# Two gate chunks moved from beside the last attention to beside the state space part

## The chip, the cores and the metric

The kernel runs on one core of a Trainium2 chip, in one launch. The metric is device microseconds of the execution, lower is better. Engines are named as in the profile: PE multiplies, PEld loads its weights, DVE, ACT and POOL work element by element, SP issues the DMA transfers.

## What is computed

Two blocks one after the other on 1024 tokens of width 1024. The first block (two layers, with a context of 256 tokens) is not touched. The second block is the reference's `second_block`:

```python
xn = rms_norm(h, mix_norm[i])
z = xn @ w_in[i]                                   # 1024 x 3072
q, k, v, gate_a, u, gate_s = jnp.split(z, splits, axis=-1)      # 512 columns each
attn = dilated_mixture_attention(q, k, v, q_norm[i], k_norm[i]) * jax.nn.silu(gate_a)
ssm = s5_glu(u, lambda_re[i], ..., b_glu[i]) * jax.nn.silu(gate_s)
h = h + jnp.concatenate([attn, ssm], axis=-1) @ w_out[i]
```

Queries and keys are normalised by head, the attention has 8 heads of 64. `s5_glu` is a linear recurrence over time in groups of 16 channels, computed as a scan, then Gelu, then a gated projection.

## The kernel before

Numbers are float32, and each product is made from a high and a low part: three matmuls (L236, L237, L238) for one. The projections of the second block go by chunks of 256 columns of `w_in`; the class `Stream` (L274 on) loads one chunk's 1 MB of weights into `raw` (one buffer), splits it into `wh` and `wl` (one set: ACT casts at L210, DVE and POOL subtract at L215, in eight pieces), and loads the next when both halves are split. `Stream.next` hands a chunk out, `Stream.ahead` splits a half of the following one as soon as its half of the set is free. The order of the chunks is the list given to `Stream`: `wspecs(w_in, a, b)` is one entry for every 256 columns.

Kinds of chunks, with the cost that the code yields for them (about a microsecond of PE per unit): queries or keys, `qk_items`, eight tiles of 128 tokens, 2.56 each, with a norm on DVE, POOL and ACT and then two transposes of 0.43 per pair of tiles (L1814), 23.9 in all; values, `v_tok`, eight tiles, 20.5; gates, `all_gates` and `gates`, two halves of 128 columns by two groups of 512 tokens, 5.12 each, 20.5 in all. A gate group is 24 matmuls of 512 columns, a Tanh on ACT (L723), a product on DVE (L724) and a store on SP (L725). The tiles `gth` and `vt` have one buffer in this part (`K.rb = 1`): the next waits for the store of the one before.

Two stages matter. In the first, `weave` runs the state space part `space()` beside the projections `proj_s()`; in the second it runs the attention `attn_s` beside `side_s()`. `weave` lets that side yield that is behind, by the numbers of `PART`: cost of the one side, cost of the other, a lead of the other, a factor on its cost. So "ssm" goes forward as 134.4 to 159 x 0.982 = 156.1. The chunks of `proj_s` are, in order: two of queries, two of keys, two of values, one of gates. `side_s` has the other three of gates, then the gated projection `glu`, a pause, and one half of the output projection; its lead of 8 puts that much of the gates ahead of the first scores.

The state space part has four blocks (`ssm`). Each counts 5 ahead of its scan (transposes and a product on PE, copied to `s_Z`), then 13 steps of 1.0 on DVE and POOL (L1740 to L1744, no PE), between which the constants of the next block are made (7 more, with some PE work), and 7 behind: products on PE (L1765, L1767), Gelu on ACT (L1769), transposes. The constants of block 0 (7) come ahead of all. The program's order is not strictly that of each engine's queue: when the kernel is built, the framework may put an instruction ahead of one that it takes for not yet ready. Each engine then works its queue in order.

Between the stages the pools change: `sp` (state space) and the six and two banks of PSUM are given up, and the attention's pool `aS` and its four and four banks take their place; the loads of keys and queries stand on SP's queue behind the stores of the values.

Of the kernel before, what the change touches and what calls it, by code (L numbers as in the profile page):

```python
# [20 lines left out]
S = 1024  # L21
# [20 lines left out]
def host_consts():  # L42
# [44 lines left out]
    "low": (27.3, 26, 1.4, 1.0),  # L87
    "m": (171, 105, 13.7, 1.0),
    "d": (176.1, 108, 8.8, 0.96),
    "ssm": (134.4, 159, 0, 0.982),  # L90
    "s": (89.1, 132, 8.0, 1.005),
}
PAUSE = {"d": 0.5, "s": 14.1, "fill": 4.0}
SSM = (2, 4, 6), (1,)
# [320 lines left out]
def wspecs(w, a, b):  # L415
    return [(w[:, c:c + 256], None) for c in range(a, b, 256)]
# [92 lines left out]
def pipe(items, filler=None, part=0.0, young=False):  # L509

    items = iter(items)
    live = []
    while True:
        it = next(items, None)
        if it is not None:
            live.append([it, 0])
        if not live:
            if filler:  # L520
                yield from filler
            return
        loads, front, chain = [], [], []
        for x in live:
            st = x[0][x[1]] or []
            if x[1] == 0:
                loads = st
            elif x[1] == 1:
                front = st
            else:  # L530
                chain = st + chain if young else chain + st
            x[1] += 1
        live = [x for x in live if x[1] < len(x[0])]
        order = [((i + 0.1) / len(front), f) for i, f in enumerate(front)] + [((i + 0.6) / len(chain), f) for i, f in enumerate(chain)]
        for _, f in sorted(order, key=lambda x: x[0]):
            c = f()
            if hasattr(c, "__next__"):
                c = yield from c
            yield c or 1e-6
        for f in loads:  # L540
            f()
        yield 1e-6
        z = 0.0
        while it is None and filler and z < part:
            x = next(filler, None)
            if x is None:
                filler = None
            else:
                z += x
                yield x  # L550
# [178 lines left out]
def all_gates(K, ws, sg, h, ntok, nf):  # L729
    for m2 in range(nf // 2):  # L730
        W = ws.next()
        for m in range(2):
            r = m2 * 2 + m
            yield from gates(K, W, sg[r * P:(r + 1) * P], h, ntok, m)
            ws.ahead(m)
# [1043 lines left out]
def qk_items(K, W, dst, h, gain):  # L1779

    nc = K.nc

    def item(t2):
        rows, st = [], []
        ss = K.small(8, "qns")

        def proj(i):
            t = t2 * 2 + i
            ps = K.w()[:, 0:256]
            c = yield from K.projy(ps, cols(h, t * P, (t + 1) * P), cols(W, 0, 256))  # L1790
            r = K.tp.tile([P, 256], F, tag="qrow", name="qrow", bufs=4)
            nc.scalar.copy(out=r, in_=ps)
            sq = K.tp.tile([P, 256], F, tag="qsq", name="qsq", bufs=2)
            nc.gpsimd.tensor_tensor(out=sq, in0=r, in1=r, op=ALU.mult)
            nc.vector.tensor_reduce(out=ss[:, i * 4:(i + 1) * 4], in_=sq.rearrange("p (h e) -> p h e", h=4), axis=AX.X, op=ALU.add)
            rows.append(r)
            return c

        def norm():
            rr = K.rsqrt(K.mean_eps(ss, 8, 64, "qnm"), 8, "qnr")  # L1800
            for i in range(2):
                r = rows[i].rearrange("p (h e) -> p h e", h=4)
                nc.vector.tensor_tensor(out=r, in0=r, in1=rr[:, i * 4:(i + 1) * 4].unsqueeze(2).to_broadcast([P, 4, 64]), op=ALU.mult)
                if gain is not None:
                    nc.gpsimd.tensor_tensor(out=r, in0=r, in1=gain.unsqueeze(1).to_broadcast([P, 4, 64]), op=ALU.mult)
                s = K.tp.tile([P, 4, 2, 64], FR, tag="qst", name="qst", bufs=2)
                K.split(s[:, :, 0, :], s[:, :, 1, :], r)
                st.append(s)

        def trans(hp):  # L1810
            ps = K.w()
            for h_ in range(2):
                for i in range(2):
                    nc.tensor.transpose(ps[:, (h_ * 2 + i) * P:(h_ * 2 + i + 1) * P], st[i].bitcast(F)[:, hp * 2 + h_].rearrange("p a e -> p (a e)"), K.ident)  # L1814
            o = K.tp.tile([P, 2, 256], F, tag="qo", name="qo", bufs=2)
            nc.scalar.copy(out=o, in_=ps.rearrange("p (h t) -> p h t", h=2))
            nc.sync.dma_start(out=dst[hp * 2:hp * 2 + 2].rearrange("h a e t -> (a e) h t")[:, :, t2 * 256:(t2 + 1) * 256], in_=o)
            return 0.43

        return [None, each(proj, 2), [norm], each(trans, 2)]  # L1820

    for t2 in range(4):
        yield item(t2)
# [179 lines left out]
def stages(K, out):  # L2003
    nc, I = K.nc, K.I
    x, xc = flat(I["x"]), flat(I["ctx"])
# [4 lines left out]
    w_in, w_out, w_ada = flat(I["ev_w_in"]), flat(I["ev_w_out"]), flat(I["ev_w_ada"])  # L2010
# [3 lines left out]
    h = [hp.tile([P, KD, T], FR, name="e_hh"), Slabs([[lo(F, k, c) for c in range(3)] for k in range(KD)], 512)]  # L2014
    rp = K.open("erp")
    ws = Stream(K, "edn", "left", 2, 2, [x for c in range(0, D, 256) for s_ in (0, D) for x in wspecs(w_ada, c + s_, c + s_ + 256)] + [
        x for i, m in enumerate([None, (w_in[:, 0:256], xy_split), (w_in[:, 256:512], xy_split)] + wspecs(w_in, 1792, 2304))
        for x in ([m] if m else []) + wspecs(w_ada, 2 * D + i * 256, min(3 * D, 2 * D + (i + 1) * 256))])
# [88 lines left out]
    for j in range(4):  # L2107
        c = 256 * j
# [27 lines left out]
    sg = [K.dram([512, T], "e_sg%d" % i) for i in range(2)]  # L2136
# [31 lines left out]
    ws = ws2  # L2168
# [121 lines left out]
    h = [hp.tile([P, KD, T], FR, name="o_h" + c) for c in "hl"]  # L2290
    w_in = flat(I["od_w_in"])
# [22 lines left out]
    qd = [K.dram([2, 2, 64, S], "o_qd%d" % i) for i in range(4)]  # L2314
    kd = [K.dram([2, 2, 64, T], "o_kd%d" % i) for i in range(4)]
    vd = [K.dram([T, 512], "o_vd%d" % i) for i in range(2)]
    sg = [K.dram([512, S], "o_sg%d" % i) for i in range(2)]
# [170 lines left out]
    w_in, w_out = flat(I["w_in_2"]), flat(I["w_out_2"])  # L2488
    hp = K.open("shT", "right")
    h = [hp.tile([P, KD, S], FR, name="s_h" + c) for c in "hl"]  # L2490
    ws = Stream(K, "sdn", "right", 1, 1, wspecs(w_in, 2048, 2560) + wspecs(w_in, 0, 2048) + wspecs(w_in, 2560, 3072))
    jk = K.open("sjk", "right")
    FG = jk.tile([P, D], F, name="o_FG")
    nc.sync.dma_start(out=FG, in_=I["final_norm_g"].unsqueeze(0).to_broadcast([P, D]))
# [29 lines left out]
            yield from ssm(K, sp, m, U[m], gT)  # L2524

    def proj_s():
        for dst, gain in ((qd, None), (kd, K.s_gain)):
            for c in range(2):
                W = ws.next()
                yield 0  # L2530
                yield from pipe(qk_items(K, W, dst[c], h, gain))
        for c in range(2):
            yield from v_tok(K, ws, vd[c], h, 8, 4, 64)
        K.tp.release()
        K.tp = K.open("stg", "right")
        yield from all_gates(K, ws, sg[0][0:256], h, S, 2)

    K.pace("ssm")
    weave(K, space(), proj_s(), *PART["ssm"])
    sp.release()  # L2540


    ap = K.open("aS")
# [3 lines left out]
    res = {}  # L2547

    def side_s():
        yield from all_gates(K, ws, sg[0][256:512], h, S, 2)  # L2550
        yield from all_gates(K, ws, sg[1], h, S, 4)
        K.tp.release()
        ws.release()
        hp.release()
        ex = res["ex"] = K.open("sow")
        parts = OutProj.parts(w_out, (1, 0))
        where = [(ex, "raw%d" % i) for i in range(2)]
        raw = [OutProj.fetch(K, where[i], parts[i]) for i in range(2)]
        ws2 = Stream(K, "sge", "right", 1, 2, wspecs(flat(I["w_glu_2"]), 0, 512), 4)
        gl = K.open("sgl", "right")  # L2560
        yield from glu(K, ws2, gl, gT, yd[1])
        gl.release()
        ws2.release()
        so = res["so"] = K.open("so", "right")
        op = res["op"] = OutProj(K, so, where, parts, raw)

        def items():
            for t in range(8):
                xr = {}

                def row(t=t, xr=xr):
                    xr[0] = so.tile([P, D], F, tag="xr", name="xr", bufs=4)
                    nc.sync.dma_start(out=xr[0], in_=x3[t * P:(t + 1) * P])

                def fin(c, ps, t=t, xr=xr):
                    nc.vector.tensor_tensor(out=xr[0][:, c:c + 512], in0=xr[0][:, c:c + 512], in1=ps, op=ALU.add)
                    if c:
                        nc.sync.dma_start(out=xa[t * P:(t + 1) * P, :], in_=xr[0])

                yield op.item(yd[1], sg[1], t, row, fin, t == 7)  # L2580

        g = pipe(items())
        next(g)
        for f in range(2):
            op.ahead(f)
        yield PAUSE["s"]
        yield from g
# [89 lines left out]
```

## Time and profile before

| | us |
|---|---|
| median of three runs | 2837.96 |
| lowest, highest | 2837.86, 2843.56 |
| the profiled execution | 2844.58 |
| its span, first to last instruction | 2842.4 |
| busy in the span: PE, DVE, ACT, POOL | 2483.3, 1745.0, 1172.7, 873.0 |
[...]

The profile is one execution. A row of the windows view gives a stretch by its ends in us from the span's start, its length, then how long each engine was busy in it with the number of its instructions, the granted clock of PE, the DMA engines' busy share and GB/s. The state space stage lies between about 2058 and 2388 us, the last attention between 2388 and 2655. Rows of the waits view give who waited for whom, us in total, times, and the longest. Rows of the timeline give start and length in us, and in brackets how long the engine was idle ahead and for whom. Matmuls are pipelined: their starts tell the pace, not their lengths.

### The profile page before, as it was taken

Reading aid. Unit: us, or ns where it says so; the run is one execution under the profiler, and the core shown is the slowest. Engines: PE = TensorE matmul, PEld = TensorE weight load, DVE = VectorE, ACT = ScalarE, POOL = GpSimd, SP = SyncE. Lnnn points to the kernel's source line nnn. Section 1 sums busy time; section 2 is a strip of 40 time slices with the busy share of each in tenths; the row PEclk is TensorE's granted clock in tenths of the full one; section 3 lists DMA queues with packets and bytes.
Section 4 is the critical chain, followed back from the end, with each engine's and each line's share of the span. In section 5 each row is a group of like instructions: output and inputs, shape, how many; then the busy total and the mean of one; then the engine's idle time right before and its main releaser. Section 6 shows DMA issues by size and latency. Waiting matters only on the chain.

```text
span 2842.4 us, 41920 instructions
## 1 busy us (share of the span) xinstructions
PE 2483.3 (87%) x14199; PEld 2092.5 (74%) x14199; DVE 1745.0 (61%) x5065; ACT 1172.7 (41%) x2589; POOL 873.0 (31%) x1157
## 2 busy tenths in 40 slices
PE   5688888779999977968999899898968879998999
PEld 4567777668877766947988777676857878877777
DVE  6643566557888977434555466667576644667643
ACT  6321455434554533323333355553423322555522
POOL 4231344310024344112122343453043432233410
PEclk9888998889999988989999999998978889999999
DMA  6236423244266444157333445566232224457521
GB/s 223 86 121 172 121 81 88 71 120 121 69 207 210 147 145 139 64 187 261 121 115 126 120 115 139 147 185 213 82 99 63 62 83 145 113 165 240 182 75 45
DMA packets 331960, 374.34 MB, mean 132 GB/s; under 512 B 39916, under 2 KB 265176, under 8 KB 331746
## 3 DMA queue, kind: packets, MB, share of 16 engines
q1 hardware_dynamic: 331586, 371.62, 43.0%
q8 instruction: 113, 1.85, 0.3%
q14 instruction: 101, 0.83, 0.1%
q10 hardware_dynamic: 160, 0.05, 0.0%
HBM read 242.59 MB, written 129.01 MB: 131 GB/s over the span
## 4 chain that ended last, share of the span: by engine, by line
PE 53%; DVE 17%; DMA 16%; POOL 4%; issue 4%; ACT 4%; SPq 1%; DVEq 0%; ACTq 0%; POOLq 0%
PE ps_w L236 9%; PE ps_w L237 9%; PE ps_w L238 9%; PE ps_w L907 5%; PE ps_w L917 3%; PE ps_w L889 2%; PE ps_w L1450 1%; PE ps_w L888 1%; DMA e_vb<-vt 1%; DVE wl L215 1%; PE ps_s L238 1%; PE ps_s L237 1%; PE ps_s L236 1%; PE ps_w L930 1%; PE ps_w L928 1%
## 5 line engine op out<-in xcount | busy, mean ns | idle before, releaser
L215 POOL TENSOR_TENSOR wl<-raw,wh 128x256 fp32r<-128x256 f32 (+1 forms) x270 | 218.4, 824 | 534.3 <-ACT wh L210 398.9
L210 ACT CAST wh<-raw 128x256 fp32r<-128x256 f32 (+1 forms) x430 | 151.9, 402 | 137.7 <-PE ps_w L237 95.9
L236 PE MATMUL ps_w<-wo_h,o_yh 128*128 128x512 f32 x416 | 178.4, 429 | 18.7 <-ACT o_yh L198 13.6
L236 PE MATMUL ps_w<-e_hh,wh 128*128 128x512 f32 (+1 forms) x480 | 181.2, 377 | 7.8 <-DVE va_t L199 7.7
L238 PE MATMUL ps_w<-wo_h,o_yl 128*128 128x512 f32 x416 | 173.0, 416 | 11.2 <-DVE o_yl L199 11.2
L238 PE MATMUL ps_w<-e_hh,wl 128*128 128x512 f32 (+1 forms) x480 | 174.9, 364 | 5.2 <-DVE wl L215 5.2
L215 DVE TENSOR_TENSOR wl<-raw,wh 128x256 fp32r<-128x256 f32 x216 | 129.8, 626 | 76.8 <-ACT wh L210 72.2
L237 PE MATMUL ps_w<-e_hl,wh 128*128 128x512 f32 (+1 forms) x480 | 174.7, 364 | 0.0
L237 PE MATMUL ps_w<-wo_l,o_yh 128*128 128x512 f32 x416 | 171.5, 412 | 0.0
L236 PE MATMUL ps_w<-wh,s_hh 128*128 128x256 f32 x512 | 153.0, 299 | 1.0 <-DVE vt L199 0.9
L237 PE MATMUL ps_w<-wl,s_hh 128*128 128x256 f32 x512 | 149.8, 293 | 0.0
L238 PE MATMUL ps_w<-wh,s_hl 128*128 128x256 f32 x512 | 149.5, 292 | 0.0
L192 DVE CUSTOM_DVE_ANT_0 b_p<-ps_w,zero 128x512 f32<-128x512 f32 (+1 forms) x192 | 109.5, 593 | 27.0 <-PE ps_w L907 27.0
L236 PE MATMUL ps_w<-o_hh,wh 128*128 128x512 f32 (+1 forms) x288 | 114.5, 398 | 8.3 <-ACT wh L210 7.3
L907 PE MATMUL ps_w<-b_k,b_q 128*128 128x512 f32 (+1 forms) x384 | 95.2, 377 | 25.1 <-DMA b_q<-e_qb 16.4
L238 PE MATMUL ps_w<-o_hh,wl 128*128 128x512 f32 (+1 forms) x288 | 113.1, 393 | 0.6 <-POOL wl L215 0.5
L237 PE MATMUL ps_w<-o_hl,wh 128*128 128x512 f32 (+1 forms) x288 | 113.1, 393 | 0.0
L999 ACT ACTIVATE b_p<-b_p,b_nm 128x1280 f32<-128x1280 f32 x64 | 87.3, 1365 | 59.5 <-DVE b_nm L998 59.1
L236 PEld LDWEIGHTS ps_w<-wo_h,o_yh 128*128 128x128 f32 x416 | 83.1, 200 | 38.1 <-ACT o_yh L198 17.8
L238 PEld LDWEIGHTS ps_w<-wo_h,o_yl 128*128 128x128 f32 x416 | 82.9, 199 | 34.9 <-DVE o_yl L199 17.4
L236 PEld LDWEIGHTS ps_w<-e_hh,wh 128*128 128x128 f32 x480 | 93.3, 194 | 19.8 <-DVE va_t L199 8.1
L238 PEld LDWEIGHTS ps_w<-e_hh,wl 128*128 128x128 f32 x480 | 93.1, 194 | 19.6 <-DVE wl L215 5.5
(533 smaller groups left out, 7834.6 us busy)
## 6 DMA issues: line engine op xcount, KB each, us to landing
raw<-in_ev_w_ada_dram SPq DMA_DIRECT2D x12, 1024.0 KB
raw<-in_ev_w_in_dram SPq DMA_DIRECT2D x12, 1024.0 KB
raw<-in_od_w_ada_dram SPq DMA_DIRECT2D x12, 1024.0 KB
raw<-in_w_in_dram SPq DMA_DIRECT2D x12, 1024.0 KB
b_k<-e_kb SPq DMA_DIRECT2D x32, 320.0 KB
raw<-in_od_w_in_dram SPq DMA_DIRECT2D x10, 1024.0 KB
d_k<-o_kd SPq DMA_DIRECT2D x32, 320.0 KB
xr<-x SPq DMA_DIRECT2D x16, 512.0 KB
```

The lines of the kernel that those rows point to most:

```text
L192: self.nc.vector.tensor_tensor_reduce(out=out, in0=ps, in1=b, scale=1.0, scalar=NEG, op0=ALU.add, op1=ALU.max, accum_out=mx)
L210: nc.scalar.copy(out=h, in_=r)
L215: (nc.vector if b == "D" else nc.gpsimd).tensor_tensor(out=l, in0=r, in1=h.bitcast(F), op=ALU.subtract)
L236: mm(out, ah, bh, start=first, stop=False)
L237: mm(out, ah, bl, start=False, stop=False)
L238: mm(out, al, bh, start=False, stop=last)
L888: mm(o[0:64, cs], v[:, 0, :], lo, start=False, stop=False)
L889: mm(o[:, cs], v.rearrange("p a e -> p (a e)"), hi, start=first, stop=last)
L907: mm(o, q, k[:, ks], start=i == 0, stop=i == n - 1)
L917: K.nc.tensor.transpose(pt[:, i * P:(i + 1) * P], p[:, (j + i) * P:(j + i + 1) * P], K.ident)
L928: mm(o, v[:, 0, :], hi[:, i, :], start=first and i == 0, stop=False)
L999: nc.scalar.activation(out=p, in_=p, func=AF.Exp, bias=nm, accum_out=den)
```

## The change

Two more of the four gate chunks go from `side_s` to `proj_s`, and the three that are there now stand between the chunks of queries and keys: query, gate, query, gate, key, gate, key, value, value. The one gate chunk that is left opens `side_s`. The list of weights follows that order. The costs of `PART` follow: 159 becomes 200, 132 becomes 91, so that "ssm" goes as 134.4 to 196.4. The gates in the first stage now take their tile from the pool `stp`, and the change to the pool `stg` moves behind the stage.

```diff
-    "ssm": (134.4, 159, 0, 0.982),
-    "s": (89.1, 132, 8.0, 1.005),
+    "ssm": (134.4, 200, 0, 0.982),
+    "s": (89.1, 91, 8.0, 1.005),
...
-    ws = Stream(K, "sdn", "right", 1, 1, wspecs(w_in, 2048, 2560) + wspecs(w_in, 0, 2048) + wspecs(w_in, 2560, 3072))
+    ws = Stream(K, "sdn", "right", 1, 1, wspecs(w_in, 2048, 2560) + [
+        x for i, c in enumerate((0, 256, 512, 768)) for y in (c, (1536, 1792, 2560, 0)[i])[:2 - i // 3] for x in wspecs(w_in, y, y + 256)] + wspecs(w_in, 1024, 1536) + wspecs(w_in, 2816, 3072))
...
     def proj_s():
-        for dst, gain in ((qd, None), (kd, K.s_gain)):
+
+        for i, (dst, gain) in enumerate(((qd, None), (kd, K.s_gain))):
             for c in range(2):
                 W = ws.next()
                 yield 0
                 yield from pipe(qk_items(K, W, dst[c], h, gain))
+                if (i, c) != (1, 1):
+                    yield from all_gates(K, ws, sg[i][c * 256:(c + 1) * 256], h, S, 2)
         for c in range(2):
             yield from v_tok(K, ws, vd[c], h, 8, 4, 64)
-        K.tp.release()
-        K.tp = K.open("stg", "right")
-        yield from all_gates(K, ws, sg[0][0:256], h, S, 2)
 
     K.pace("ssm")
     weave(K, space(), proj_s(), *PART["ssm"])
     sp.release()
+    K.tp.release()
+    K.tp = K.open("stg", "right")
...
     def side_s():
-        yield from all_gates(K, ws, sg[0][256:512], h, S, 2)
-        yield from all_gates(K, ws, sg[1], h, S, 4)
+        yield from all_gates(K, ws, sg[1][256:512], h, S, 2)
         K.tp.release()
```

## Rows read from the trace of the kernel before

**Rows 1.** The page's first line.

```profile
span 2842.4 us, 41920 instructions
```

**Rows 2.** Windows view, the last attention in six stretches, with the columns' names.

```profile
core 0: us, PE busy (x) PEld busy (x) DVE busy (x) ACT busy (x) POOL busy (x), PEclk, DMA share, GB/s
2388.00:2411.00 23.00, 22.96 (x103) 18.81 (x102) 6.31 (x16) 7.19 (x15) 3.12 (x4) 0.99 0.74 224
2411.00:2511.00 100.00, 99.69 (x523) 80.73 (x522) 61.72 (x180) 55.49 (x130) 25.26 (x36) 1.00 0.42 118
2511.00:2521.00 10.00, 5.91 (x24) 4.33 (x23) 8.43 (x11) 7.20 (x12) 5.29 (x4) 0.87 0.83 231
2521.00:2551.00 30.00, 30.00 (x159) 24.37 (x158) 18.26 (x53) 18.59 (x41) 11.00 (x16) 0.99 0.50 165
2551.00:2575.00 24.00, 17.73 (x92) 13.18 (x91) 21.54 (x53) 16.57 (x38) 12.52 (x13) 0.96 0.85 252
2575.00:2655.00 80.00, 78.23 (x401) 62.95 (x400) 52.17 (x135) 40.66 (x87) 26.61 (x29) 0.97 0.70 217
```

**Rows 3.** Windows view, state space stage: its four scans, then two stretches between them.

```profile
2099.00:2128.00 29.00, 18.62 (x127) 17.44 (x127) 27.35 (x97) 9.31 (x24) 15.12 (x22) 0.79 0.23 73
2177.00:2202.00 25.00, 14.71 (x105) 14.37 (x104) 21.90 (x73) 5.92 (x15) 12.11 (x19) 0.80 0.26 85
2267.00:2294.00 27.00, 12.86 (x91) 11.68 (x91) 24.74 (x86) 7.65 (x21) 15.14 (x24) 0.73 0.27 90
2340.00:2361.00 21.00, 20.14 (x168) 19.94 (x168) 17.75 (x55) 1.87 (x5) 8.00 (x13) 1.00 0.29 101
2128.00:2177.00 49.00, 47.00 (x351) 42.83 (x351) 29.47 (x85) 18.32 (x38) 15.39 (x18) 0.88 0.25 70
2202.00:2267.00 65.00, 58.12 (x410) 52.32 (x409) 42.43 (x125) 22.31 (x50) 27.51 (x35) 0.84 0.21 60
```

**Rows 4.** Waits view, 2080 to 2385 us: two of PE, one of ACT.

```profile
PE ps_w L1814 <- DVE qst L199: 27.9, 10, 10.3
...
ACT vt L198 <- DMA s_vd<-vt: 27.1, 10, 4.9
...
PE ps_s L1767 <- DVE s_Z L1743: 11.4, 2, 7.2
```

**Rows 5.** Timeline of PE, end of the second query chunk, start of the first key chunk.

```profile
2188.75 1.99 PE L1814 MATMUL ps_w<-ident,qst 128*128 128x128 f32 x8 [10.29 <-DVE qst L199]
2190.40 0.56 PE L236 MATMUL ps_w<-wh,s_hh 128*128 128x256 f32 x1
```

**Rows 6.** Timeline of PE: first gate matmuls behind the values; seven gate matmuls later.

```profile
2365.85 0.50 PE L236 MATMUL ps_w<-s_hh,wh 128*128 128x512 f32 x1 [1.23 <-ACT wh L210]
...
2398.01 0.39 PE L237 MATMUL ps_w<-s_hl,wh 128*128 128x512 f32 x1
...
2399.37 0.39 PE L237 MATMUL ps_w<-s_hl,wh 128*128 128x512 f32 x1
```

**Rows 7.** Groups by line and shape, 2391 to 2515 us: the gates' product on DVE.

```profile
L724 DVE SCALAR_TENSOR_TENSOR gth<-gth,ps_w 128x512 f32<-128x512 f32 x15 | 10.3, 687 | 23.4 <-ACT gth L723 23.4
```

**Rows 8.** Timelines of SP's queue and of PE: last value store, first scores.

```profile
2381.67 0.32 SPq L698 DMA_DIRECT2D s_vd<-vt  x1
...
2408.68 0.62 PE L1867 MATMUL ps_s<-s_k,s_q 128*128 128x128 f32 x4
```

**Rows 9.** Groups of ACT by line, whole span: the table load at Gelu.

```profile
L1769 ACT ACT_TABLE_LOAD x1 | 1.3, 1283 | 0.0
```

**Rows 10.** Timeline of ACT: last Gelu, first Tanh of the gates.

```profile
2384.02 0.60 ACT L1769 ACTIVATE s_Y<-ps_s 128x512 f32<-128x512 f32 x1 [2.84 <-PE ps_s L1767]
...
2388.70 0.66 ACT L723 ACTIVATE gth<-ps_w 128x512 f32<-128x512 f32 x1
```

**Rows 11.** Windows view, two stretches of earlier stages with a full DVE.

```profile
960.00:980.00 20.00, 18.14 (x118) 15.07 (x119) 19.28 (x60) 9.39 (x20) 8.47 (x7) 1.00 0.53 172
1960.00:1980.00 20.00, 14.82 (x51) 11.14 (x52) 18.45 (x51) 7.35 (x14) 2.56 (x2) 0.83 0.53 170
```

## Prediction

> **What bounds the kernel now.** I read the page's head for the span [rows 1], then the two stages that the change touches, each cut into stretches [rows 2, 3], then what PE waits for in the first of them [rows 4, 5], and last the single instructions and stretches that give a price [rows 6 to 11]. In [rows 2] the reader is to see that the last attention is bound by PE: in its first 100 us, where gate chunks run beside it, PE is busy for 99.69 us at clock 1.00, and in the whole 267 us it is idle for 12.5. In [rows 3] he is to see that the state space stage is not bound by one engine. Three stretches are scans (2099 to 2128, 2177 to 2202, 2267 to 2294), with queries and keys on PE: DVE is busy for 27.35 of 29, 21.90 of 25 and 24.74 of 27 us, PE for only 18.62, 14.71 and 12.86, at a granted clock of 0.73 to 0.80. That is 10.4 + 10.3 + 14.1 = 34.8 us of idle PE. The fourth scan (2340 to 2361) runs beside value tiles, which need little of DVE: there PE is busy for 20.14 of 21 us at 1.00. The stretches between them lose 2.0 and 6.9 us. The waits agree: 27.9 us of PE's transposes for the split rows of queries and keys, 11.4 for the end of a scan [rows 4]; the longest is 10.29 us [rows 5].
>
> **What the change moves.** By the costs in the code a chunk of queries or keys counts 23.9, a gate or value chunk 20.5; a block of the state space part counts 5 ahead of its scan, 20 in it (13 in the last block) and 7 behind it. Before, the two sides go forward as 134.4 to 156.1, so the scans lie at 13-36, 50-73, 87-110 and 124-139 of the projections, and the chunks at q 0-48, k 48-96, v 96-137, gate from 137: three scans beside queries and keys (the third partly beside values). After, they go as 134.4 to 196.4: scans at 16-45, 63-92, 110-139 and 156-175, gate chunks at 24-44, 68-89 and 113-133, values from 157. So each of three scans lies mostly beside a gate chunk and the fourth beside values, which is the state of the good stretch of [rows 3].
>
> **The sum, step by step**, against the profiled execution (2844.58 us, its span 2842.4 and 2.2 around it; the median of the runs is 2837.96, 0.23% lower).
>
> 1. *Out of the last attention.* A gate chunk is 96 matmuls of 512 columns (8 parts x 3 products x 4 groups), and they start 0.23 us apart at clock 1.00 [rows 6], 1.36 us for six: 21.8 us a chunk, 43.6 for two. PE is full there [rows 2], so this comes off: -43.6.
>
> 2. *What is late next in the attention.* Its own work now gets less PE work beside it, and DVE moves up. DVE's 168.4 us in that stage (the sum of [rows 2]) lose 8 x 0.687 for the gates [rows 7] and a little for weight splits: 163 or less in about 223. Nearest rows: PE stayed busy for 18.14 of 20 us beside 19.28 of DVE in one stretch, and only for 14.82 beside 18.45 in another [rows 11]. At the first row's loss (9%) over the 45 us or so where DVE would be that full the price is 4; at the second's (26%) it is 12; at none it is 0. I take 4, since the average of 73% is well below both rows.
>
> 3. *The hand-over to the attention.* Before, a whole gate chunk lies between the last values and the attention's pools. ACT is late there, because each value tile waits for the store of the one before (27.1 us, 10 times [rows 4]), the last store is issued at 2381.67, and PE is fed by gates until the first scores at 2408.68 [rows 8]. After, values end the stage; the keys' loads are behind the last value store on SP's queue, and PE has one gate chunk (21.8 us) for the gap of 27 us between that store and the scores. The uncovered part is about 5 us; 0 if all of the chunk fits in, 16 if the scores are queued after the lead of 8 (8.5 us of gates) and the chunk's rest behind them. I take 5. The gate stores themselves (one 256 KB store per group on SP) stay as many as before, only earlier.
>
> 4. *Into the state space stage.* The same 96 matmuls twice: +43.6 at full clock. Their tanh and product (4 each a chunk) find ACT and DVE free once the scan is alone with them. Their two weight loads of 1 MB go from SP's queue in the attention to the queue here, where the DMA engines are 0.21 to 0.29 busy [rows 3]: no price.
>
> 5. *Three more changes of weights.* One set of weights, so a new chunk waits for the split of its own. The change from values to gates cost PE 1.23 us [rows 6]; by three that is 3.7, twice as much if the scan holds DVE and POOL. I take 6. It was covered by attention before.
>
> 6. *What the gates fill.* Below: nothing, if PE's tail of each query or key chunk, its last transposes waiting behind norm and scan, stays as in [rows 5] (4 x 10.3 = 41 against the 34.8 now). Above: all 34.8, and with it the half-speed work. In the three scans 46.2 us of busy PE at 0.73 to 0.80 are 10.4 us lost to the lower of the two clock levels, and the stretches behind them (47.0 at 0.88, 58.12 at 0.84 [rows 3]) lose 15 more; 60 in all. The wait for the scan's end (11.4 [rows 4]) goes for sure, since PE has gates until then. I take 4 tails of 5 us in place of 34.8, -15, and 10 of the 25 of clock: -25. The row behind that is the fourth scan's.
>
> Sum: -43.6 + 4 + 5 + 43.6 + 6 - 25 = **-10**, 2834.6 against the profile, 2828 against the median.
>
> [...]
>
> **The rivals.**
> - *All of it filled* (term 6 at -45 to -50): -33, 2811.6 against the profile, so 2805. For it: the fourth scan's row. Against it: gates come after the last transposes in the program, as the next chunk does now, whose matmuls start behind them in [rows 5].
> - *The tail stays in front* (slower). The transposes of the last rows of each chunk stand ahead of the gate matmuls in PE's queue; scans begin just at these tails (63 against 68, 110 against 113, 156 against 157), so all four look like the 10.29 of [rows 5]. It decides from the point where more than 10 us of each of the four tails is idle: then term 6 is only the 11.4 of the scan's end, of which some goes back, say -7, and terms 2, 3 and 5 at 4, 8 and 7 remain: +12, 2856.6 against the profile, so 2850.
> - *Nothing to be told apart*: PE's work is only carried from one place to another, and term 6 just pays terms 2, 3 and 5 (15 us): 2838. The order in each queue is fixed when the kernel is built, so that the gates do not come to lie beside the scans at all belongs here too.
> - *Table loads.* ACT would alternate between Gelu (four blocks) and Tanh (three chunks). The trace has one load at the first Gelu, 1.283 us, and the gates' Tanh at 2388.70 follows the Gelu of 2384.02 with none [rows 9, 10]: price 0. If each change loaded, six loads were 7.7 us of ACT, and if all of it held PE 2836. [...]
>
> **How the numbers follow.** Forecast 0.38, all filled 0.15, tail in front 0.26, nothing 0.18, table loads 0.03. The forecast's own range is 2818 to 2834, of which a tenth is within 0.2%. The measurement tells about 0.2% (5.7 us) from no change: below 2832.3 is faster, above 2843.6 slower. Faster: 0.15 + 0.9 x 0.38 + a little of "nothing" (0.03) = 0.52; slower: 0.26 + 0.01 = 0.27; same: the rest, 0.21. Likeliest case's time 2828. The range takes in the rivals up to 2851 and down to 2803: beyond it are the full 60 of term 6 and term 3 at 16 together with the tails.
>
> **What would show it.** In the profile of the changed kernel: three gate chunks beside scans, with PE above 90% and clock near 1.00 there; no PE wait for the scan's end; the attention shorter by 35 to 44 us; the state space stage longer by 20 to 35. Wrong would be: PE waits of 10 us for split rows at each chunk's end, ahead of gate matmuls (the tail); PE idle ahead of the first scores by more than 10 us (term 3); a load of tables at each Gelu; PE below 85% in the attention with DVE above 90% (term 2).

## The result, and the profile after

The changed kernel takes 2858.56 us in the median, the kernel before beside it on the same chip 2839.57: ratio 1.0057, 95% interval 1.0035 to 1.0079. It is slower by 0.57%, where 2828 was forecast, and the time lies above the range. The profiled execution takes 2858.89 us; its head, which answers to [rows 1]:

```profile
span 2857.1 us, 41915 instructions
```

Where the time went is read by cutting both traces at the first scores and at the last ones (L1867). Windows view of the kernel before: first stage from 2050 us on, attention, the rest (stretch, length, then busy us and instructions of PE, PEld, DVE, ACT, POOL, then clock, DMA share and GB/s):

```profile
2050.00:2408.70 358.70, 294.51 (x2034) 265.27 (x2033) 209.71 (x605) 103.33 (x235) 127.30 (x172) 0.85 0.29 86
2408.70:2639.40 230.70, 218.46 (x1125) 175.21 (x1124) 153.38 (x415) 131.93 (x294) 78.28 (x94) 0.98 0.58 174
2639.40:2842.40 203.00, 186.83 (x839) 148.93 (x837) 94.72 (x174) 65.51 (x123) 33.17 (x24) 0.98 0.30 98
```

The same of the changed kernel:

```profile
2050.00:2456.40 406.40, 329.55 (x2206) 294.66 (x2204) 220.03 (x621) 114.65 (x257) 133.42 (x180) 0.87 0.27 82
2456.40:2652.70 196.30, 179.90 (x941) 142.60 (x942) 142.44 (x400) 120.79 (x271) 71.45 (x86) 0.97 0.66 195
2652.70:2857.10 204.40, 186.84 (x830) 148.40 (x828) 91.54 (x172) 65.17 (x122) 34.00 (x24) 0.97 0.29 94
```

The first stage is 47.7 us longer, the attention only 34.4 shorter, the rest 1.4 longer: +14.7 of span. In the first stage PE is busy for 35.0 us more and idle for 12.7 more (76.9 against 64.2). Idle time was to be filled there; there is more of it.

The scans show why. Windows view of the changed kernel: its four scans, then two of the gate chunks, in answer to [rows 3]:

```profile
2101.00:2131.00 30.00, 16.70 (x126) 15.89 (x124) 28.75 (x103) 9.02 (x24) 15.04 (x22) 0.82 0.33 105
2194.00:2223.00 29.00, 13.97 (x104) 13.14 (x103) 26.95 (x94) 9.07 (x24) 13.34 (x21) 0.76 0.27 91
2280.00:2310.00 30.00, 17.23 (x106) 15.68 (x105) 28.77 (x92) 8.89 (x22) 16.60 (x24) 0.72 0.27 88
2366.00:2393.00 27.00, 15.47 (x100) 14.53 (x99) 24.94 (x77) 8.30 (x21) 15.58 (x23) 0.68 0.30 98
2224.00:2251.00 27.00, 27.00 (x137) 21.79 (x136) 12.05 (x19) 7.42 (x16) 8.03 (x9) 0.96 0.17 54
2305.00:2332.00 27.00, 27.00 (x137) 21.98 (x136) 11.82 (x17) 7.54 (x17) 8.86 (x9) 0.94 0.14 49
```

DVE is nearly full in the scans (92 to 96%) and PE about half idle; in the gate chunks PE is full and DVE under half busy. The two hardly overlap: the gates begin at 2135.1, 2223.5 and 2305.4, and the last operations of the scans ahead of them at 2130.8, 2222.3 and 2309.4. The fourth scan, which was good before, has become like the others (15.47 of 27 busy, clock 0.68). The timeline of PE in the changed kernel, from the end of the second query chunk to its gate chunk, shows what lies between:

```profile
2204.00 0.28 PE L238 MATMUL ps_w<-wh,s_hl 128*128 128x256 f32 x1
2207.76 0.33 PE L1814 MATMUL ps_w<-ident,qst 128*128 128x128 f32 x1 [3.47 <-DVE qst L199]
2208.86 1.67 PE L1814 MATMUL ps_w<-ident,qst 128*128 128x128 f32 x7 [0.77 <-DVE qst L199]
2210.32 0.64 PE L1765 MATMUL ps_s<-s_TT,s_UT 128*128 128x128 f32 x2
2221.73 2.09 PE L1814 MATMUL ps_w<-ident,qst 128*128 128x128 f32 x8 [10.78 <-DVE qst L199]
2223.47 0.78 PE L236 MATMUL ps_w<-s_hh,wh 128*128 128x512 f32 x1
```

And the timeline of DVE, the first and the last step of the second scan, and between them rows of the norm (`qns`, `qnm`, `qnri`, then the split `qst`) among rows of the scan (`s_Z`):

```profile
2193.67 0.69 DVE L1740 TENSOR_TENSOR sc_t<-s_Z,s_Ap 128x512 f32<-128x512 f32 x1
...
2212.97 0.41 DVE L1795 TENSOR_REDUCE qns<-qsq 128x4 f32<-128x256 f32 x1
...
2213.45 0.15 DVE L186 TENSOR_SCALAR qnm<-qns 128x8 f32<-128x8 f32 x1
2213.64 0.20 DVE L1743 TENSOR_TENSOR s_Z<-s_Z,sc_t 128x28 f32<-128x28 f32 x1
2213.75 0.16 DVE L171 TENSOR_SCALAR qnri<-qnm 128x8 int32<-128x8 int32 x1
...
2221.27 0.75 DVE L199 TENSOR_TENSOR qst<-qrow,qst 128x256 fp32r<-128x256 f32 x2
...
2222.27 0.41 DVE L1744 TENSOR_TENSOR s_Z<-s_Z,sc_t 128x252 f32<-128x252 f32 x1
```

From the last query matmul at 2204.00 to the first gate matmul at 2223.47 PE does only transposes and two of the block's products. The rows for them come out of DVE between scan steps, the last just as the scan ends. This is [rows 5] again, with gates behind the wait in place of keys. The waits view of the changed kernel, 2080 to 2460 us, in answer to [rows 4]:

```profile
PE ps_w L1814 <- DVE qst L199: 43.1, 10, 10.8
...
PE ps_s L1767 <- DVE s_Z L1743: 9.4, 1, 9.4
```

The wait for split rows rose from 27.9 to 43.1 us, and that for a scan's end is still there. In the attention PE waits for the row maxima and, just ahead of the first scores, for a load of keys (waits view of the changed kernel, 2456.4 to 2652.7, then of the kernel before, 2408.7 to 2639.4):

```profile
PE ps_s L1867 <- DVE s_mx L192: 8.5, 11, 3.0
...
PE ps_s L1867 <- DMA s_k<-s_kd: 3.3, 1, 3.3
```

```profile
PE ps_s L1867 <- DVE s_mx L192: 3.5, 3, 1.4
```

### The profile page after: what moved, and what is told of

Same layout as the page of the kernel before. It is cut to its first block, busy times and chain, and to the rows that moved or that the text cites. A ratio compares the mean times of both kernels' runs of the same rounds, so it can differ in the third digit from the quotient of the medians.

```text
span 2857.1 us, 41915 instructions
## 1 busy us (share of the span) xinstructions
PE 2480.6 (87%) x14199; PEld 2091.2 (73%) x14199; DVE 1741.1 (61%) x5065; ACT 1172.5 (41%) x2589; POOL 871.3 (30%) x1157
## 4 chain that ended last, share of the span: by engine, by line
PE 54%; DVE 17%; DMA 15%; POOL 5%; issue 4%; ACT 4%; SPq 1%; DVEq 0%; ACTq 0%; POOLq 0%
PE ps_w L236 9%; PE ps_w L237 9%; PE ps_w L238 9%; PE ps_w L907 5%; PE ps_w L917 3%; PE ps_w L889 2%; PE ps_w L1450 1%; DVE wl L215 1%; DMA e_vb<-vt 1%; PE ps_w L928 1%; PE ps_w L930 1%; PE ps_w L888 1%; PE ps_w L929 1%; PE ps_s L238 1%; PE ps_s L237 1%
## 5 line engine op out<-in xcount | busy, mean ns | idle before, releaser
L215 POOL TENSOR_TENSOR wl<-raw,wh 128x256 fp32r<-128x256 f32 (+1 forms) x270 | 218.8, 826 | 565.7 <-ACT wh L210 431.4
L236 PE MATMUL ps_w<-wo_h,o_yh 128*128 128x512 f32 x416 | 179.2, 431 | 14.0 <-ACT o_yh L198 9.1
L236 PE MATMUL ps_w<-e_hh,wh 128*128 128x512 f32 (+1 forms) x480 | 181.0, 377 | 7.8 <-DVE va_t L199 7.6
L215 DVE TENSOR_TENSOR wl<-raw,wh 128x256 fp32r<-128x256 f32 x216 | 130.9, 630 | 72.9 <-ACT wh L210 68.5
L237 PE MATMUL ps_w<-e_hl,wh 128*128 128x512 f32 (+1 forms) x480 | 174.7, 364 | 0.0
L237 PE MATMUL ps_w<-wo_l,o_yh 128*128 128x512 f32 x416 | 171.9, 413 | 0.0
L236 PE MATMUL ps_w<-wh,s_hh 128*128 128x256 f32 x512 | 150.7, 294 | 0.2 <-DVE s_hl L579 0.2
L237 PE MATMUL ps_w<-wl,s_hh 128*128 128x256 f32 x512 | 148.2, 289 | 0.1
L236 PE MATMUL ps_w<-o_hh,wh 128*128 128x512 f32 (+1 forms) x288 | 115.1, 400 | 8.0 <-ACT wh L210 7.2
L237 PE MATMUL ps_w<-o_hl,wh 128*128 128x512 f32 (+1 forms) x288 | 113.4, 394 | 0.0
L236 PEld LDWEIGHTS ps_w<-e_hh,wh 128*128 128x128 f32 x480 | 93.5, 195 | 19.8 <-DVE va_t L199 8.0
L236 PEld LDWEIGHTS ps_w<-wo_h,o_yh 128*128 128x128 f32 x416 | 83.5, 201 | 33.4 <-ACT o_yh L198 13.2
```

The lines of the kernel that those rows point to most:

```text
L215: (nc.vector if b == "D" else nc.gpsimd).tensor_tensor(out=l, in0=r, in1=h.bitcast(F), op=ALU.subtract)
L236: mm(out, ah, bh, start=first, stop=False)
L237: mm(out, ah, bl, start=False, stop=False)
```

## The experiments

Theory A: the tail of each query or key chunk stands ahead of the gates in PE's queue, and the scan on DVE holds it up. Its rivals are named in the expectations. A table of what all kernels gave comes first. "First stage" runs from 2050 us to the first scores, "idle" is PE's in it, both from windows like those above; the ratios are to the kernel before beside them. Single executions of one kernel differ by several us (the six of the changed kernel lie between 2850.50 and 2861.95), so stage lengths carry less than ratios.

| kernel | ratio, 95% interval | first stage | idle | attention |
|---|---|---|---|---|
| before | 1 | 358.7 | 64.2 | 230.7 |
| changed | 1.0057 (1.0035 to 1.0079) | 406.4 | 76.9 | 196.3 |
| changed, gates at the end | 1.0048 (1.0030 to 1.0067) | 404.3 | 67.1 | 193.6 |
| changed, lead 10 | 0.9976 (0.9965 to 0.9987) | 384.4 | 60.0 | 197.3 |
| changed, lead 20 | 0.9959 (0.9945 to 0.9974) | 372.9 | 53.2 | 196.1 |
| changed, pipeline | 0.9961 (0.9947 to 0.9974) | 378.5 | 53.6 | 197.9 |
| changed, both | 0.9938 (0.9917 to 0.9960) | 360.4 | 43.5 | 200.0 |
| changed, both, values too | 0.9933 (0.9911 to 0.9955) | 354.6 | 36.1 | 197.3 |
| before, pipeline | 1.0000 (0.9988 to 1.0012) | 354.7 | 60.3 | 229.9 |
| before, lead 10 | 0.9982 (0.9971 to 0.9993) | 338.8 | 57.2 | 229.5 |
| before, both | 0.9946 (0.9931 to 0.9961) | 332.9 | 49.7 | 229.5 |
| before, both, values too | 0.9961 (0.9945 to 0.9977) | 333.9 | 44.4 | 230.3 |
| half the move, both, values too | 0.9984 (0.9968 to 0.9999) | 353.8 | 42.7 | 218.4 |
| changed, no scans | 0.9866 (0.9846 to 0.9886) | 346.0 | 30.5 | 195.2 |

**Gates at the end: the move without the interleaving.**

```diff
-                if (i, c) != (1, 1):
-                    yield from all_gates(K, ws, sg[i][c * 256:(c + 1) * 256], h, S, 2)
...
             yield from v_tok(K, ws, vd[c], h, 8, 4, 64)
+        yield from all_gates(K, ws, sg[0], h, S, 4)
+        yield from all_gates(K, ws, sg[1][0:256], h, S, 2)
```

> The changed kernel with the same three gate chunks in the first stage, but behind the values and not between the queries and keys: the move alone without the interleaving. Theory A: the interleaving as it was built brings nothing, since the tails stay in front; so this is as slow as the changed kernel or up to 8 us better, as the gates at the end cover the hand-over: 2848 to 2860. If the interleaving does fill scans, by 15 to 25 us as forecast, this one is slower than the changed kernel by that: 2870 to 2885.

The list of weights is in the old order here. 2852.86 us, 1.0048: as theory A has it. Putting the gates between the chunks, the part of the change that was to bring the gain, brought nothing that can be measured; PE's waits for rows are 24.6 us here, against 43.1 with the gates between.

**One pipeline.** Queries, gates and keys become items of one `pipe`, so that a chunk's norm and last transposes come behind the first gate groups; `Late` takes a chunk's weights when its first matmul is issued.

```diff
-                W = ws.next()
-                yield 0
-                yield from pipe(qk_items(K, W, dst[c], h, gain))
-                if (i, c) != (1, 1):
-                    yield from all_gates(K, ws, sg[i][c * 256:(c + 1) * 256], h, S, 2)
+                    yield from qk_items(K, Late(ws), dst[c], h, gain)
+                    if (i, c) != (1, 1):
+                        yield from gate_items(K, ws, sg[i][c * 256:(c + 1) * 256], h, S)
+        yield from pipe(items())
```

> The changed kernel with the chunks of queries, gates and keys in one pipeline: the norm and the last transposes of a chunk now stand behind the first one and two gate groups and not ahead of all of them; the places of the scans and all work stay. Theory A: the waits of PE for split rows at the first three tails (6.6, 15 and 12.8 us) nearly go, the fourth ahead of the values stays (11.4), and the time is 20 to 30 us below the changed kernel, 2828 to 2838. Theory B: the same 2853 to 2863. Between them, if the weights' split of the gate chunk, which shares DVE with the scan, is late instead: PE waits for wh or wl appear in place of the waits for the rows, and the time falls by under 10.

2831.59 us, ratio 0.9961, 27 us below the changed kernel. PE's waits in it, 2060 to 2400 us, are:

```profile
PE ps_w L1814 <- DVE qst L199: 14.5, 5, 8.9
...
PE ps_w L236 <- ACT wh L210: 3.4, 1, 3.4
...
PE ps_w L238 <- POOL wl L215: 2.4, 2, 2.2
```

The wait for rows fell by 28.6 us, the longest that is left stands ahead of the values, the wait for the first scan's end (9.4) is gone too, and a small part came back as waits for the gates' weights. Theory A holds for what the change cost, and theory B, that the loss lies at the hand-over and in the attention, falls.

**The same pipeline without gates**, in the kernel before:

```diff
-                W = ws.next()
-                yield 0
-                yield from pipe(qk_items(K, W, dst[c], h, gain))
+                    yield from qk_items(K, Late(ws), dst[c], h, gain)
+        yield from pipe(items())
```

> The kernel before with its four chunks of queries and keys in one pipeline (the tail of a chunk stands behind the first tiles of the next); no gate is moved. Theory A, that the tails cost the idle PE wherever they stand ahead of other matmuls: the 27.9 us of waits for split rows fall to 10 to 15 and the time by 8 to 15 us below the kernel before, 2823 to 2831. Theory C, that only work without a need of DVE can fill a scan (the next query tiles need the same DVE, so the wait moves on to their rows or to the buffers of four rows): within 4 us of the kernel before.

Ratio 1.0000: theory C by its time. PE's waits for rows fell from 27.9 to 18.5 us, but 10.9 us of waits for the split weights of the next chunk (L236 and L237 on `wh` and `wl`) stand where 1.2 were, a wait that theory C had not named. The two results together: behind a tail the order alone is worth nothing when the next chunk is one of queries or keys, and about 1% with gates.

**A lead of 10** for the projections, in the changed kernel:

```diff
-    "ssm": (134.4, 200, 0, 0.982),
+    "ssm": (134.4, 200, 10, 0.982),
```

> The changed kernel with one number altered: the state space part starts 10 units of projection work later (the lead in the first stage's entry goes from 0 to 10), so each scan should start when the last transposes of a query or key chunk are issued and not half a chunk ahead of them. Theory A (the tail stays in front: the last rows of a chunk are normed between the steps of a scan on DVE, and PE's gate matmuls stand behind their transposes): PE's wait for split rows falls from 43 us to under 15, the wait for the scan's end to about 0, the time by 20 to 35 us below the changed kernel, to 2824 to 2838. Theory B (the loss lies at the hand-over and in the denser attention, the scans' place does not matter): within 5 us of the changed kernel, 2853 to 2863.

2834.49 us, within theory A's figure, but not by its mechanism. The waits view, 2060 to 2400 us:

```profile
PE ps_w L1814 <- DVE qst L199: 44.3, 12, 10.5
...
PE ps_w L1668 <- POOL sc_aB L1624: 2.1, 1, 2.1
```

The wait for rows stayed. What went is a wait for the constants at the stage's start (14.4 us in the changed kernel) and that for the first scan's end (9.4). Whether this needs the gates, the same lead in the kernel before tells:

```diff
-    "ssm": (134.4, 159, 0, 0.982),
+    "ssm": (134.4, 159, 10, 0.982),
```

> The kernel before with the lead of 10 alone; no gate is moved. In the run of the changed kernel with this lead the waits for split rows did not fall (44.3 us); what went was PE's wait for the constants at the stage's start (14.4 to 2.1 us) and that for the end of the first scan (9.4 to 0). The kernel before has both waits too (14.3 and, for two scans, 11.4). Theory D (the lead's gain has nothing to do with the gates): 10 to 20 us below the kernel before, 2818 to 2829. Theory A (the lead helps because gates then fill the scans): within 5 us of the kernel before.

Ratio 0.9982, 5 us: at theory A's edge. The start's wait fell here too (14.3 to 2.2) and the waits for scans' ends (11.4) are gone, but the wait for rows rose from 27.9 to 36.1 us. By these rows the start is a gain of its own, of which the kernel before loses most again at its tails.

**A lead of 20**, in the changed kernel, which puts the first three scans behind the tails:

```diff
-    "ssm": (134.4, 200, 0, 0.982),
+    "ssm": (134.4, 200, 20, 0.982),
```

> The changed kernel with a lead of 20, so that a scan begins about 10 units behind the end of a query or key chunk and not at its tail. Theory A in its strict form (the tail is long because scan steps stand between the norm's): PE's last wait of each tail falls from 8 to 10 us to under 4, 44 us of waits for split rows to under 20. Theory A2 (the chain of the norm, some 20 small instructions on DVE with ACT and POOL in between, is 5 to 7 us long by itself, and only the rest is the scan): each last wait stays at 5 to 7 us, the sum at 25 to 32. The time by A 2815 to 2825, by A2 2825 to 2838.

2824.65 us, at the border of the two theories' times, and 28.0 us of waits for rows: theory A2 by the waits. The last waits of three tails are 6.95, 7.58 and 11.37 us (the first tail has none over 1.5), the longest at the fourth tail, where the scan begins at the tail again (2338.41). The other three scans lie wholly or for the greater part beside gates now, and what the forecast counted on holds there: in the second, from 2190.6 to 2212.0, PE is busy for 19.42 of 21.4 us, its gate matmuls 0.23 us apart, beside 19.1 of DVE. At the second tail, whose scan starts only at 2190.61, the timeline of PE in this kernel shows the last query matmul and the last transposes:

```profile
2172.59 0.28 PE L238 MATMUL ps_w<-wh,s_hl 128*128 128x256 f32 x1
...
2180.70 2.14 PE L1814 MATMUL ps_w<-ident,qst 128*128 128x128 f32 x8 [6.95 <-DVE qst L199]
```

Between them the timeline of POOL has:

```profile
2172.27 3.16 POOL L215 TENSOR_TENSOR wl<-raw,wh 128x256 fp32r<-128x256 f32 x4 [4.74 <-ACT wh L210]
2175.40 0.61 POOL L1794 TENSOR_TENSOR qsq<-qrow 128x256 f32<-128x256 f32 x1
```

and then that of DVE:

```profile
2176.49 0.17 DVE L186 TENSOR_SCALAR qnm<-qns 128x8 f32<-128x8 f32 x1
...
2179.13 0.17 DVE L180 SCALAR_TENSOR_TENSOR qnry<-qnrb,qnry 128x8 f32<-128x8 f32 x1
2179.33 0.76 DVE L1803 TENSOR_TENSOR qrow<-qrow,qnry 128x256 f32<-128x256 f32 x2
2180.22 0.82 DVE L199 TENSOR_TENSOR qst<-qrow,qst 128x256 fp32r<-128x256 f32 x2
```

With no scan in it, a tail is 8 us long: the square waits on POOL behind 3.16 us of weight splits for the next chunk, then 2.84 us of DVE go to the inverse root (L186 to L180, 0.17 us each, about 0.2 apart, on 8 elements), then the product, the split and the transposes. An instruction on 8 elements took 0.17 us in these rows, the sum over 256 (L1795 of the same tail) 0.42.

**No scans.** Of each step in `ssm` all is left out but one addition in the first and the last step:

```diff
-        x1 = t1([P, 2, R, 64], "sc_t1")[:, :, :, :cnt]
-        x2 = t1([P, 2, R, 64], "sc_t2")[:, :, :, :cnt]
...
+        if i > 0:
+            return
...
+        nc.vector.tensor_tensor(out=both, in0=both, in1=both, op=ALU.add)
```

> The changed kernel without the scans: of the five operations of each step all are left out, but for one addition in the first and in the last step of each block, so the recurrence is not computed; the constants and all of PE's work stay. It shows how long a tail is without scan steps between the norm's instructions. Theory A in its strict form: the last wait of each of the four tails (0.9, 10.8, 7.2 and 8.9 us) falls under 4 us. Theory A2 (the norm's own chain sets it): the last waits stay at 5 to 7 us, 20 to 28 in all. The time is below the changed kernel by what the scans cost it: by A about 35 to 45 us, 2813 to 2823; by A2 15 to 25 us, the wait for the scan's end (9.4) and the scans' share of the tails, 2833 to 2843.

2796.44 us, 1.9% below the changed kernel, more than either theory gave, and only 2.8 us of waits for rows. By that number the strict theory A would stand; PE's timeline speaks against it:

```profile
2179.03 1.04 PE L1814 MATMUL ps_w<-ident,qst 128*128 128x128 f32 x8
...
2185.85 0.49 PE L1765 MATMUL ps_s<-s_TT,s_UT 128*128 128x128 f32 x2
2187.15 1.97 PE L1814 MATMUL ps_w<-ident,qst 128*128 128x128 f32 x8 [0.82 <-DVE qst L199]
```

The last rows still come 8 us behind the last matmul (2187.15). But the block's products (L1765 and L1767), which have no scan to wait for now, run in that gap. So the tail's own chain is 8 us here too, and the scan stretches it: in the changed kernel the second tail lasts from 2204.0 to 2221.7, 17.7 us. Of these 9.0 pass before the last sum of squares (2212.97), against 3.5 with the lead of 20: ACT copies the last rows only at 2209.24, behind the rows before, whose product it awaits from DVE. Then the inverse root takes 5.7 us in place of 2.84, with scan steps between its own.

**Both cures, with the move and without it**: the diffs of the pipeline and of the lead of 10 together, in the changed kernel and in the kernel before.

> The changed kernel with both: the lead of 10, and queries, gates and keys in one pipeline. If the two cures are of different waits (the constants at the start and the first scan's end; the three tails), their gains over the changed kernel (about 23 and 27 us) add up, less the 9.4 of the first scan's end that both take: 2858 - 41 = 2817, 2812 to 2824. If they are of the same idle time: 2828 to 2833.

> The kernel before with the lead of 10 and its four chunks of queries and keys in one pipeline; no gate is moved. Beside the changed kernel with the same two cures this tells what the move of the gates is worth once nothing else stands in its way. If gates fill scans as the forecast had it (10 to 15 us), this one is that much slower than the changed kernel with both: 2827 to 2835. If the move itself is worth nothing or less, because the attention gives back only about 34 of 43.6 us, it is as fast or faster: 2810 to 2822.

0.9938 with the move, 0.9946 without. Most of both gains comes through: 1.2% from the changed kernel, where one alone gave 0.8 and the other 1.0, less the 9.4 us (0.3%) that both take. The move by itself is then worth nothing that can be told apart. Its first stage is 27.5 us longer (360.4 against 332.9), its attention 29.5 shorter. The forecast's terms for the first stage (43.6 + 5 + 6 - 25) add up to 29.6: with both cures on either side that sum comes true, and it is the attention that gives back too little for the forecast's gain.

**Values in the pipeline too**, with the move, without it, and with half of it. To the kernels with both cures comes

```diff
+            for c in range(2):
+                yield from v_items(K, ws, vd[c], h)
         yield from pipe(items())
-        for c in range(2):
-            yield from v_tok(K, ws, vd[c], h, 8, 4, 64)
```

where `v_items` yields the tiles of `v_tok` two by two. For half the move there is besides

```diff
-    "ssm": (134.4, 200, 10, 0.982),
-    "s": (89.1, 91, 8.0, 1.005),
+    "ssm": (134.4, 179.5, 10, 0.982),
+    "s": (89.1, 111.5, 8.0, 1.005),
...
-                    if (i, c) != (1, 1):
-                        yield from gate_items(K, ws, sg[i][c * 256:(c + 1) * 256], h, S)
+                    if c == 0:
+                        yield from gate_items(K, ws, sg[0][i * 256:(i + 1) * 256], h, S)
...
-        yield from all_gates(K, ws, sg[1][256:512], h, S, 2)
+        yield from all_gates(K, ws, sg[1], h, S, 4)
```

with the list of weights in the order of the chunks.

> The changed kernel with the lead of 10 and all chunks of the first stage in one pipeline, the values too, so that the last tail (11.4 us of PE waits for split rows, ahead of the values) has value tiles ahead of it. If a tail is covered by any matmuls that stand ahead of it: 8 to 11 us below the kernel with queries, gates and keys in the pipeline, 2808 to 2812 on the profile's scale, ratio to the kernel before 0.990 to 0.992. If the wait only moves (to the split of the values' weights, which shares DVE, POOL and ACT with the fourth scan): within 4 us of it, ratio 0.993 to 0.995.

> The same for the kernel before: lead of 10, queries, keys and values in one pipeline, one gate chunk at the stage's end, three in the attention; no gate is moved. With queries and keys alone in the pipeline it was about as fast as the changed kernel with the same (0.9946 and 0.9938). If the move is worth nothing by itself, the two stay within 0.2% of each other here as well, both at 0.990 to 0.993; if gates beside scans are worth the forecast's 10 us, this one is 0.3 to 0.4% behind.

> Half the move, with the same two cures: query, gate, query, key, gate, key, value, value in one pipeline with the lead of 10, and two gate chunks left beside the attention. If the first stage fills the same share of each gate chunk and the attention gives back the same share, this lies between the two others, all within 0.2%. If the first chunk moved fills idle time (about 8 us each) and the second finds none left, or if the attention gives back the first chunk in full (21.8) and less of the second, this is the fastest of the three, by 4 to 8 us.

0.9933 with the move, the fastest that computes everything; 0.9961 without; half the move 0.9984. The second result is what neither reading of its expectation had: the two are 0.28% apart, more than the 0.2% of a worthless move and just under the 0.3 to 0.4% of the forecast's 10 us. The intervals overlap, and the pair before was 0.08% apart, so it stays open whether the move is worth up to those 10 us once the tails are covered. With the move no tail is left. The waits view, 2060 to 2400 us:

```profile
PE ps_w L237 <- POOL wl L215: 8.4, 6, 2.1
...
PE ps_w L237 <- DVE wl L215: 3.8, 3, 1.9
...
PE ps_w L238 <- DVE wl L215: 2.8, 3, 1.3
...
PE ps_w L236 <- ACT wh L210: 1.8, 3, 1.2
...
PE ps_w L1814 <- DVE qst L199: 0.5, 1, 0.5
```

Against the kernel with queries, gates and keys in the pipeline the ratio (0.9933 and 0.9938) is that of the second expectation, the span of the profiled execution (2805.5 and 2813.4) that of the first; the wait for split weights, 16.8 us, is next, and it does not come from the move: without it the same waits are 17.6. Half the move is neither between the others nor the fastest, as its two readings would have it, but the slowest: its attention gives back 12 us of 21.8, and PE waits 5.7 us for one set of weights ahead of the values. Why the dose does not count evenly stays open.

## Why the prediction was wrong

The step that failed is the reckoning by cost units and, built on it, term 6: -25 was forecast, about +1 came. By the units the second scan was to begin 5 units ahead of its gate chunk (63 against 68) and so to lie "mostly beside a gate chunk". But the units count PE's work alone; while PE stands at the transposes (10.78 us at the second tail) its place in the order does not advance and DVE's does. And in DVE's queue the norm that the transposes wait for stands step by step among the scan's steps (2213.45 to 2221.27), though `qk_items` gives it out in one piece. So the scan is over when PE gets to the gates: 2193.7 to 2222.7 against the gates from 2223.5. What sets that order when the kernel is built was not tried.

- *Terms 1 and 2, 43.6 out of the attention, 4 for its denser rest.* The direction was right, the second part too small: the attention is 34.4 us shorter, so its price is 9.2, within the 0 to 12 given. PE is idle for 16.4 us against 12.2 there, with waits for row maxima of 8.5 against 3.5; the rest is busy time, 38.6 less in place of 43.6, at a clock of 0.97 for 0.98. The waits from DVE came with DVE at 73% (142.44 of 196.3), the average that had been taken to keep the price low. The seven kernels with the whole move and all scans give back 31 to 37; what slows the busy part was not tried.
- *Term 3, the hand-over, 5.* PE waits 3.3 us for keys. Right.
- *Term 4, into the first stage, 43.6*: right as the work; what it costs there is term 6.
- *Term 5, weight changes, 6.* Nothing: no wait for `wh` or `wl` is among PE's in the first stage, as the splits lie in the tails' idle time (at the second tail, 2204.0 to 2221.7, the eight pieces of L215 lie between 2207.57 and 2215.03). With the tails gone such waits show, but no more of them with the move than without (16.8 and 17.6 us): mis-sized either way.
- *Term 6, what the gates fill, -25.* The first stage grew by 47.7 = 43.6 + 3.3 + 0 + 0.8: term 6 was about +1. Its clock part came, 8.6 for the 10 forecast (35.0 us more of busy PE in place of 43.6, at a mean granted clock of 0.87 for 0.85). The filling, -15, turned into +9.4 us of idle time: waits for rows +15.2, the scans' end -2.0, smaller ones -3.8. That the wait for the scan's end "goes for sure" was wrong: the first block's products stand ahead of the first gates in the queue (9.4 us). Behind the second scan they come after the gates (2255.78) and do not wait, as meant.
- *The rest of the kernel*, 1.4, had no term.

The rival *the tail stays in front* is what happened, by its mechanism: waits of 10.8, 7.2 and 8.9 us at three of four tails, and 9.4 for the scan's end at the first. It was priced at 2850, and 12 us against the profile; 14.3 came. That the sum is so near is in part luck: the attention cost 5.2 us more than its term, the first stage 3.9 less than the rival's terms for it, and 1.4 had no term. *Nothing to be told apart* is out by the interval, but what it says of the queues, that the gates may not come to lie beside the scans at all, is what the rows show. The text even had the rival's sign in hand, scans that begin "just at these tails", and the row of the key chunk's matmuls behind their transposes; yet the likelier case was taken from the fourth scan, whose values have no tail. That row showed what PE does beside a scan when nothing stands ahead, not what happens behind a tail.

*Table loads* is out, as forecast. Timeline of ACT in the changed kernel, its only load at a Gelu; a Tanh stands just ahead of it, and behind it Gelu and Tanh alternate up to 2349.93 without another load:

```profile
2163.10 0.59 ACT L723 ACTIVATE gth<-ps_w 128x512 f32<-128x512 f32 x1
2163.71 1.28 ACT L1769 ACT_TABLE_LOAD   x1
2165.55 0.60 ACT L1769 ACTIVATE s_Y<-ps_s 128x512 f32<-128x512 f32 x1 [0.55 <-PE ps_s L1767]
```

*All of it filled* did not come in any kernel tried: with both cures and the values in the pipeline PE is still idle for 36.1 us in the first stage, and of that kernel's 0.9933 the cures without the move give 0.9961.

## What to carry to other kernels

Work without a need of the busy engine filled a stretch here only where it stood ahead, in its own engine's queue, of whatever waits for that busy engine: with the gates behind the last transposes PE waited 43.1 us for rows, with gate groups ahead of them 14.5. So look at what closes the piece of work in front, and let the filler go between that piece's last input and its tail. A place in a plan by cost units is not a place in time: at the second tail PE's units stood still for 10.78 us while the scan went on. Before a filler is moved, price what it leaves: here the attention gave back 31 to 37 of 43.6 us, so the move had to fill 7 to 13 before it was worth anything.

## What the runs showed of the hardware

Behind the second tail's wait PE started at about half its later pace. After the 10.78 us the gate matmuls of 512 columns started 0.43 us apart from 2224.05 to 2225.75, then 0.23 apart; the granted clock is 0.51 from 2223.47 to 2226.13 and 1.00 from there to 2228.87. Here in the timeline of the changed kernel:

```profile
2224.47 0.63 PE L238 MATMUL ps_w<-s_hh,wl 128*128 128x512 f32 x1
2224.90 0.63 PE L236 MATMUL ps_w<-s_hh,wh 128*128 128x512 f32 x1
...
2229.33 0.39 PE L238 MATMUL ps_w<-s_hh,wl 128*128 128x512 f32 x1
2229.55 0.39 PE L236 MATMUL ps_w<-s_hh,wh 128*128 128x512 f32 x1
```

So this tail cost 1.3 us more behind its end: six matmuls took 2.66 us where six at the later pace took 1.4. Term 6 speaks of two clock levels. Around the 10.29 us of [rows 5], in steps of one microsecond, the granted clock of the kernel before is 1.00 in each from 2177 to 2183, 0.50 in each from 2184 to 2194 and 1.00 in each from 2195 to 2207; only in the two steps between it lies between the two values (0.90 and 0.98).

The mean granted clock of the first stage, with PE's idle time in it, is 0.87 with 76.9 us in the changed kernel, 0.92 with 53.2 at lead 20, 0.92 with 43.5 with both cures, 0.94 with 36.1 with the values too, and 0.93 with 30.5 without the scans. The kernel before has 0.85 with 64.2.

The time of one and the same kernel scatters: twelve executions of the kernel before with a lead of 10 lie between 2825.93 and 2839.79 us, 0.5% apart, the fastest at a mean clock of 0.937, the slowest at 0.932.
